# The first norm of a streaming-encoder block: products with diagonals of the tokens' factors in place of a scaled copy and transposes

## The chip, the core and the metric

The kernel runs on one core of one Trainium2 chip. The metric is the device time of one execution in microseconds (us), lower is better. A core has TensorE (PE, matrix products; its weight loads are shown as PEld), VectorE (DVE), ScalarE (ACT), GpSimd (POOL) and SyncE (SP, which here only issues DMAs). Each engine works through its own queue in order; semaphores tie them together.

## The reference

One layer of a hybrid encoder on 1024 tokens of 1024 channels, in float32:

```python
x = x + 0.5 * swiglu(rmsnorm(x, ffn1_norm), ffn1_w_gate, ffn1_w_up, ffn1_w_down)
# then a mixing block (gated gMLP heads and gated DeltaNet heads), added to x,
# a second SwiGLU half step, and a last RMSNorm
def rmsnorm(x, g):      # per token, over the 1024 channels
    return x * rsqrt(mean(x * x) + 1e-6) * g
def swiglu(x, w_gate, w_up, w_down):     # 2816 hidden channels
    return (silu(x @ w_gate) * (x @ w_up)) @ w_down
```

The change concerns the first `rmsnorm` and the way in which its result reaches the first `swiglu`. A norm has two kinds of factors: one for each token, `rsqrt(...)`, and one for each channel, `g`.

## The kernel before, in words

**The first FFN.** Products run on float32 data split into a high part, rounded to a shorter format (a cast on ACT), and a low part, the rest (a subtraction on DVE); three products of parts make one (`mm3`, line 55). The operands lie channel-major: 128 channels on the partitions, tokens along the row. The 2816 hidden channels are worked in 22 chunks of 128. Chunks 1 to 21 (`gu`, line 249) use a Strassen-like scheme with seven products in place of eight. Its blocks go by token halves and channel halves: the left half of the tokens are tiles 0 to 3 (a tile has 128 tokens), the right half tiles 4 to 7, and the channels are split at 512. So each product of such a chunk runs over four channel blocks k, on 512 columns. It needs, on the activation side, the blocks called B11, B21 and B22 and the sums T1 = B12 - B11, T2 = B22 - T1, T3 = T2 - B11 and T4 = B21 - T2, each as a high and a low part; on the weight side, four sums on POOL (`s1` to `s4`) and seven splits (`load_gu`, line 181). Chunk 0 (`gu_plain`, line 229) uses plain products on B11, B12, B21 and B22, without T sums, in two halves: columns 0 to 255 and columns 256 to 511. A column stands for one token of the left and one of the right half, so the first of these halves needs tiles 0, 1, 4, 5 and the second tiles 2, 3, 6, 7.

**The start of the program** is `start1` (line 467). For tiles 0, 4, 1, 5: ACT squares the tile and sums it along the row (line 74), DVE scales the sum and adds the epsilon (line 76), POOL takes the power -0.5 (line 70), and DVE multiplies the tile in place with the token factor and the norm row (line 82). The norm row is broadcast to 128 partitions by a DMA of 512 KB (`grow`, line 64). Then, for each pair of tiles (i, i + 4), `Combos.blocks` (line 127) transposes four channel blocks of 128x128 into one PSUM bank of 512 columns (`transposed`, line 92), four banks for each pair. From each bank ACT casts the high parts (lines 118 and 141), DVE subtracts for the low parts (lines 119 and 142), and unsplit copies for the T sums are taken off as well (lines 133, 137, 148, 150). The second half's norm treats its four tiles as one: four squares (line 488), one scaling (line 490), one power, four multiplies (line 493). At the end, `put_sums` (line 153) splits T2, T1, T3 and T4 for each of the four pairs: 16 casts of 128x512 on ACT, eight subtractions on DVE, eight on POOL, and four unsplit differences for T3 on POOL (line 157). After `start1`, the loop at line 311 prepares chunk 1's weights and runs it, and so on.

**What sets the order.** A scheduler that runs when the program is built fixes each engine's queue: written order gives the priority, and an instruction whose inputs it holds to be ready may pass one that is written earlier. Tiles of one tag share a number of buffers: the tag `x` has 8 (x tiles, later the unsplit f tiles, the gated hidden values and the loads of the down projection), `graw` 4 (raw gate and up weights), `gsp` 7 (split weights, B12, scratch), `sf` 4 (weight sums). PSUM has two sets of four banks, `mm` and `ax`. Chunk 0 uses `mm`, the transposes and chunk 1 use `ax`.

Of the kernel before, what the change touches and what calls it, by code (L numbers as in the profile page):

```python
# [30 lines left out]
def block_kernel(ctx: ExitStack, tc, a, out):  # L31
# [75 lines left out]
    class Combos:  # L107
        def __init__(self, g, qp, bp):
            self.g, self.qp, self.bp, self.B, self.f = g, qp, bp, {}, {}

        def put(self, n, i, src, eng):
# [5 lines left out]
            t = self.B[n][:, :, :, i * P:i * P + P]  # L117
            nc.scalar.copy(t[:, 0], src)  # L118
            eng.tensor_tensor(t[:, 1], src, t[:, 0], op=ALU.subtract)  # L119
# [7 lines left out]
        def blocks(self, i, pp, xns, uv, b12=None):  # L127
# [23 lines left out]
            yield  # L151

# [12 lines left out]
    def ffn(cb, wgu, wd, ps, rp, gp, qp, bp, start, load_xts, emit, before={}, fill=None):  # L165
# [145 lines left out]
        for c in range(1, NCH):  # L311
            together(load_gu(c))
            if c % 2:
                weight_sums(c // 2)
            else:
                hidden_sums(c // 2 - 1)
            gu(c, (A, X)[c % 2])
            for f in before.get(c, ()):
                f(xts)
# [125 lines left out]
    ba = cp.tile([P, 16, 8], F32, tag="ba", name="ba")[:, :8]  # L445
# [9 lines left out]
    xs = load_x(xdram, (0, 4))  # L455
    g = grow("ffn1_norm")
    xs.update(load_x(xdram, (1, 5)))

    with ExitStack() as f1:
# [5 lines left out]
        cb = Combos(g, qp, bp)  # L465

        def start1(f):
            def xi(i):
                return xs[i], xs[i + 4]

            uv = [cb.sums() for _ in range(2)]
            for j in range(2):
                for i in range(2):
                    normed(xi(i)[j], g, xi(i)[j], uv[i][j])
            def b12():
                return [f.gtile(F32R, "B12").rearrange("p s (k n) -> p s k n", k=2) for _ in range(2)]

            weights = f.load_gu(0, True)
            next(weights)
            xs.update(load_x(xdram, (2, 6, 3, 7)))  # L480
            b = b12()
            parts = [cb.blocks(i, f.X, xi(i), uv[i], b) for i in range(2)]
            together(*parts, n=2)
            together(*parts, weights)
            rest = xi(2) + xi(3)
            ms = sm.tile([P, 4], F32, tag="ssk", name="ms4")
            for i, x in enumerate(rest):
                nc.scalar.activation(f.gtile(F32, "junk").rearrange("p s n -> p (s n)"), x, AF.Square, accum_out=ms[:, i:i + 1])
            rs = sm.tile([P, 4], F32, tag="rk", name="rs4")
            nc.vector.tensor_scalar(rs, ms, 1.0 / D, EPS, op0=ALU.mult, op1=ALU.add)  # L490
            rpow(rs, rs, 4)
            for i, x in enumerate(rest):
                nc.vector.scalar_tensor_tensor(x, x, rs[:, i:i + 1], g, op0=ALU.mult, op1=ALU.mult)
            f.gu_plain(slice(0, 256), b)
            b = b12()
            for i in range(2, 4):
                together(cb.blocks(i, f.X, xi(i), cb.sums(xp), b))
            f.gu_plain(slice(256, 512), b)
            V, G = nc.vector, nc.gpsimd
            together(*(cb.put_sums(i, ("T2", "T1", "T3", "T4"), (V, G, V, G)) for i in range(4)))  # L500
# [57 lines left out]
    with ExitStack() as f2:  # L558
# [37 lines left out]
        cb = Combos(g2, qp, bp)  # L596
# [660 lines left out]
def _layout(np, x, ffn1_norm, ffn1_w_gate, ffn1_w_up, ffn1_w_down, mix_norm, w_in, gm_ln_g, gm_ln_b, gm_w_s,  # L1257
# [6 lines left out]
    def tmaj(cols):  # L1264
# [7 lines left out]
        x=x, ffn1_norm=ffn1_norm, mix_norm=mix_norm, ffn2_norm=ffn2_norm, final_norm=final_norm.reshape(1, D),  # L1272
# [34 lines left out]
```

## Time and profile before

| | |
|---|---|
| median of 3 timed runs | 1852.29 us (1849.4 to 1852.42) |
| the profiled execution | 1841.22 us, of which the profile's span is 1839.4 us |
| busy share of the span | PE 97%, DVE 65%, POOL 41%, ACT 37% |
| mean granted TensorE clock | 0.992 of full speed |
| moved by DMA | 302 MB, 164 GB/s on average |

Times in the profile are microseconds from the start of the span. A line such as L62 is a line of the kernel before; where it is that of a helper, the names of the written and read tiles tell the use: `out<-in`. "x1056" is a count. What follows a "|" in a group's row is busy time in us and the mean ns of one, then the engine's idle time just before them and what ended it. In rows of stretches, the numbers with (x...) are busy us and instructions of PE, PEld, DVE, ACT and POOL; then come the granted TensorE clock, the DMA engines' share and GB/s. In the chain of waits each row is a start, a length and what the time was spent on. The rows themselves are shown in the prediction.

### The profile page before, as it was taken

To read this page: it belongs to the slowest core of one execution; us is meant where nothing else is said; L and a number is where in the kernel's file an instruction comes from. 1 tells how busy PE (TensorE), PEld (TensorE's weight loads), DVE (VectorE), ACT (ScalarE), POOL (GpSimd) and SP (SyncE) were. 2 spreads that over 40 slices of the span, in tenths; PEclk is the share of its full clock that TensorE was granted. 3 is DMA by queue.
4 is the path that set the end of the run, shared out by engine and by line. 5 is a ranking of instruction groups with operands and counts; after the bars stand their busy time and mean duration, and the time that the engine had idled before them with its cause. 6 is when DMAs were issued, how large, how long until landed. Compare 5 with 4: busy or idle time off the path is not lost.

```text
span 1839.4 us, 25484 instructions
## 1 busy us (share of the span) xinstructions
PE 1784.1 (97%) x9735; PEld 1524.8 (83%) x9735; DVE 1191.7 (65%) x1531; ACT 686.6 (37%) x1193; POOL 747.9 (41%) x583
## 2 busy tenths in 40 slices
PE   5999999999999999898999999999999999999997
PEld 4888888888788889797788989988888888878886
DVE  6867676665565575769655344587776766656546
ACT  6333332333343454432344533452333323243433
POOL 4667666565140012212132420366666665614001
PEclk9999999999999999999999999999999999999999
DMA  5353443544957445453432254334535445495744
GB/s 196 108 175 136 162 152 134 184 158 163 339 188 258 155 177 164 140 195 100 133 94 67 90 197 136 109 104 165 178 132 171 144 154 188 142 344 185 264 142 149
DMA packets 134441, 302.26 MB, mean 164 GB/s; under 512 B 27408, under 2 KB 42032, under 8 KB 134320
## 3 DMA queue, kind: packets, MB, share of 16 engines
q1 hardware_dynamic: 131824, 296.20, 46.9%
q10 hardware_dynamic: 2496, 4.44, 0.8%
q8 instruction: 76, 1.25, 0.3%
q14 instruction: 45, 0.37, 0.1%
HBM read 208.83 MB, written 91.77 MB: 163 GB/s over the span
## 4 chain that ended last, share of the span: by engine, by line
PE 78%; DVE 8%; DMA 5%; POOL 4%; issue 3%; ACT 2%; SPq 0%; POOLq 0%; DVEq 0%; ACTq 0%
PE mm L53 43%; PE ax L53 32%; POOL s L191 1%; POOL t L278 1%; DMA left<-hq 1%; DVE acc L873 1%; PE ax L95 1%; PE sd L53 1%; DMA graw<-in_f1gu_dram 1%; POOL s L278 1%; PE sc L53 1%; DVE T L119 0%; DVE unit L62 0%; DVE wk L62 0%; DVE E L797 0%
## 5 line engine op out<-in xcount | busy, mean ns | idle before, releaser
L53 PE MATMUL mm<-unit 128*128 128x512 f32 x1056 | 244.9, 392 | 4.2 <-ACT unit L61 2.2
L53 PEld LDWEIGHTS mm<-unit 128*128 128x128 f32 x1056 | 198.8, 189 | 47.4 <-ACT unit L61 3.3
L191 POOL TENSOR_TENSOR s<-graw 128x512 f32<-128x512 f32 x84 | 130.3, 1551 | 262.9 <-DMA graw<-in_f2gu_dram 116.0
L62 DVE TENSOR_TENSOR ga<-graw,ga 128x512 fp32r<-128x512 f32 x134 | 155.9, 1166 | 99.9 <-ACT ga L61 99.2
L61 ACT CAST gs<-s 128x512 fp32r<-128x512 f32 x168 | 104.5, 622 | 301.8 <-PE mm L53 151.0
L62 DVE TENSOR_TENSOR unit<-left,unit 128x1024 fp32r<-128x1024 f32 x84 | 101.9, 1215 | 133.0 <-ACT unit L61 132.3
L53 PE MATMUL ax<-T,gs 128*128 128x512 f32 x792 | 183.1, 389 | 0.0
L53 PE MATMUL ax<-unit 128*128 128x512 f32 x792 | 180.5, 389 | 0.0
L53 PEld LDWEIGHTS ax<-T,gs 128*128 128x128 f32 x792 | 148.7, 188 | 30.8
L53 PEld LDWEIGHTS ax<-unit 128*128 128x128 f32 x792 | 148.7, 188 | 30.8
L62 DVE TENSOR_TENSOR gs<-s,gs 128x512 fp32r<-128x512 f32 x168 | 172.7, 1030 | 2.3
L53 PE MATMUL mm<-B,ga 128*128 128x512 f32 (+1 forms) x864 | 166.8, 347 | 3.3 <-ACT B L118 1.9
L61 ACT CAST unit<-left 128x1024 fp32r<-128x1024 f32 x84 | 82.5, 982 | 230.2 <-PE ax L53 100.5
L53 PE MATMUL mm<-T,gs 128*128 128x512 f32 x720 | 166.5, 389 | 0.0
L53 PEld LDWEIGHTS mm<-B,ga 128*128 128x128 f32 x864 | 139.5, 194 | 23.4 <-ACT B L118 2.5
L53 PEld LDWEIGHTS mm<-T,gs 128*128 128x128 f32 x720 | 135.2, 188 | 28.0
L70 POOL TENSOR_TENSOR rs<-rs,half 128x1 f32<-128x1 f32 (+1 forms) x29 | 19.2, 662 | 334.5 <-DVE rs L76 334.4
L53 PE MATMUL mm<-actT,wk 128*128 128x512 f32 x576 | 150.4, 403 | 0.0
L53 PE MATMUL ax<-B,ga 128*128 128x512 f32 x528 | 127.2, 390 | 1.4 <-DVE ga L62 1.4
L53 PE MATMUL mm<-wk,actT 128*128 128x256 f32 x960 | 123.5, 285 | 2.7 <-DVE wk L62 2.7
L53 PEld LDWEIGHTS mm<-wk,actT 128*128 128x128 f32 x960 | 117.4, 190 | 3.4 <-DVE wk L62 3.0
L53 PEld LDWEIGHTS mm<-actT,wk 128*128 128x128 f32 x576 | 103.6, 188 | 18.8
(239 smaller groups left out, 3046.0 us busy)
## 6 DMA issues: line engine op xcount, KB each, us to landing
left<-hq SPq DMA_DIRECT2D x70, 512.0 KB, 5.0
graw<-in_f1gu_dram SPq DMA_DIRECT2D x44, 512.0 KB, 5.4
wq<-t SPq DMA_DIRECT2D x44, 512.0 KB, 2.8
hq<-s SPq DMA_DIRECT2D x44, 512.0 KB, 3.1
graw<-in_f2gu_dram SPq DMA_DIRECT2D x44, 512.0 KB, 4.7
right<-wq SPq DMA_DIRECT2D x40, 512.0 KB, 4.8
wd<-in_f1wd_dram SPq DMA_DIRECT2D x22, 512.0 KB, 6.6
hq<-sg SPq DMA_DIRECT2D x22, 512.0 KB, 3.7
```

The costliest lines, as they stand in the source:

```text
L53: nc.tensor.matmul(*args, **kw)
L61: nc.scalar.copy(h, src)
L62: nc.vector.tensor_tensor(l, src, h, op=ALU.subtract)
L70: nc.gpsimd.tensor_tensor(o, i, half[:, :w], op=ALU.pow)
L95: nc.tensor.transpose(ps[:, i * P:(i + 1) * P], blk(i), ident)
L191: nc.gpsimd.tensor_tensor(f, u, v, op=op)
L278: nc.gpsimd.tensor_tensor(o, u, v, op=op)
L873: nc.vector.scalar_tensor_tensor(acc, pad[:, j:j + 512], cw[:, blk, j:j + 1], acc, op0=ALU.mult, op1=ALU.add)
```

## The change

For the first norm, the scaled copy of x and the transposes are left out. A product of a raw x block (128 tokens by 128 channels, as the stationary operand) with a diagonal matrix of 128 token factors yields the block transposed and scaled by token, in one step. The channel factors `g` now lie one to a partition after that product, so they are applied in the evictions from PSUM: ACT's cast gets a factor per partition (`nc.scalar.mul`), and DVE's subtraction becomes a multiply and subtract in one instruction (`scalar_tensor_tensor`).

- The norm's channel factors come as a 128x8 array (4 KB) in place of the row broadcast to 128 partitions.
- `factors` does four tiles at once for either half: four squares on ACT (with the 1/1024 folded into their scale), an add and a power on POOL, and four products of the identity with a token factor on DVE, which make the diagonals.
- `scaled_blocks` goes by channel blocks: for each of eight blocks, four products fill a bank with tiles 0, 1, 4, 5 (or 2, 3, 6, 7), and the evictions are 128x256: three casts or copies on ACT and three on DVE for blocks 0 to 3, two and four for blocks 4 to 7. Before, a bank held four channel blocks of one tile, and the evictions were 128x512.
- The second half's factors are asked for before chunk 0's products on the first half (before: four tiles' squares and power stood there too, with the four multiplies).
- The unsplit f tiles of the second half lie in three buffers of `x` and one of `graw`.
- `scaled_sums` makes the T sums for 256 columns at once: eight casts of 128x1024 (as 4x256) in place of 16 of 128x512, and likewise the subtractions.
- Chunk 1's weights (`load_gu(1)`) are prepared in turns with the T sums; before, they followed them.

```diff
+        def scaled_blocks(self, i, pp, xts, dg, g, f, b12):
+            sl = slice(i * 256, i * 256 + 256)
+            t3, t1, t2, t4 = self.f[i] = f
+            def less(o, src, c, v):
+                nc.vector.scalar_tensor_tensor(o, src, g[:, c:c + 1], v, op0=ALU.mult, op1=ALU.subtract)
+            def put(h, l, src, c):
+                nc.scalar.mul(h, src, g[:, c:c + 1])
+                less(l, src, c, h)
+            for c in range(8):
+                ps = bank(*pp)
+                for n, x in enumerate(xts):
+                    mm(ps[:, n * P:n * P + P], x[:, c * P:c * P + P], dg[:, n * P:n * P + P], start=True, stop=True)
+                u, v = ps[:, :256], ps[:, 256:]
+                k = c % 4
+                if c < 4:
+                    b = self.block("B11")
+                    put(b[:, 0, k, sl], b[:, 1, k, sl], u, c)
+                    nc.scalar.mul(t3[:, k], u, g[:, c:c + 1])
+                    b = b12[k // 2]
+                    put(b[:, 0, k % 2], b[:, 1, k % 2], v, c)
+                    less(t1[:, k], v, c, t3[:, k])
+                else:
+                    b = self.block("B21")
+                    put(b[:, 0, k, sl], b[:, 1, k, sl], u, c)
+                    b = self.block("B22")
+                    put(b[:, 0, k, sl], b[:, 1, k, sl], v, c)
+                    less(t2[:, k], v, c, t1[:, k])
+                    less(t4[:, k], u, c, t2[:, k])
+                yield
+        def scaled_sums(self, i, names, engs):
+            t3, t1, t2, t4 = self.f[i]
+            for n, eng in zip(names, engs):
+                if n == "T3":
+                    nc.gpsimd.tensor_tensor(t3, t2, t3, op=ALU.subtract)
+                src, t = {"T1": t1, "T2": t2, "T3": t3, "T4": t4}[n], self.block(n)[:, :, :, i * 256:i * 256 + 256]
+                nc.scalar.copy(t[:, 0], src)
+                eng.tensor_tensor(t[:, 1], src, t[:, 0], op=ALU.subtract)
+                yield
...
         for c in range(1, NCH):
-            together(load_gu(c))
+            if c not in gu_s:
+                together(load_gu(c))
...
-    xs = load_x(xdram, (0, 4))
-    g = grow("ffn1_norm")
-    xs.update(load_x(xdram, (1, 5)))
+    nc.scalar.dma_start(g1, a["f1g"])
+    xs = load_x(xdram, (0, 1, 4, 5))
...
-            for j in range(2):
-                for i in range(2):
-                    normed(xi(i)[j], g, xi(i)[j], uv[i][j])
...
+            order = ((0, 1, 4, 5), (2, 3, 6, 7))
+            def factors(ts):
+                ms, rs = (sm.tile([P, 4], F32, tag=n, name=n) for n in ("ssk", "rk"))
+                for n, t in enumerate(ts):
+                    junk = f.gtile(F32, "junk").rearrange("p s n -> p (s n)")
+                    nc.scalar.activation(junk, xs[t], AF.Square, scale=D ** -0.5, accum_out=ms[:, n:n + 1])
+                nc.gpsimd.tensor_scalar(rs, ms, EPS, None, op0=ALU.add)
+                rpow(rs, rs, 4)
+                dg = rp.tile([P, 544], F32, tag="sf", name="dg", bufs=4)[:, :512]
+                for n in range(4):
+                    nc.vector.tensor_scalar(dg[:, n * P:n * P + P], ident, rs[:, n:n + 1], None, op0=ALU.mult)
+                return dg
...
             weights = f.load_gu(0, True)
+            dg = factors(order[0])
             next(weights)
-            xs.update(load_x(xdram, (2, 6, 3, 7)))
+            xs.update(load_x(xdram, order[1]))
             b = b12()
-            parts = [cb.blocks(i, f.X, xi(i), uv[i], b) for i in range(2)]
-            together(*parts, n=2)
-            together(*parts, weights)
-            rest = xi(2) + xi(3)
...
-            for i, x in enumerate(rest):
-                nc.vector.scalar_tensor_tensor(x, x, rs[:, i:i + 1], g, op0=ALU.mult, op1=ALU.mult)
+            together(cb.scaled_blocks(0, f.X, [xs[t] for t in order[0]], dg, g1, four(cb.sums() + cb.sums()), b), weights)
+            dg = factors(order[1])
             f.gu_plain(slice(0, 256), b)
             b = b12()
-            for i in range(2, 4):
-                together(cb.blocks(i, f.X, xi(i), cb.sums(xp), b))
+            t4 = rp.tile([P, 1088], F32, tag="graw", name="t4", bufs=4)[:, :D].rearrange("p (a n) -> p a n", a=2)
+            fs = four([xp.tile([P, 2, 512], F32, tag="x", name="f") for _ in range(3)] + [t4])
+            together(cb.scaled_blocks(1, f.X, [xs[t] for t in order[1]], dg, g1, fs, b))
             f.gu_plain(slice(256, 512), b)
             V, G = nc.vector, nc.gpsimd
-            together(*(cb.put_sums(i, ("T2", "T1", "T3", "T4"), (V, G, V, G)) for i in range(4)))
+            together(f.load_gu(1), *(cb.scaled_sums(i, ("T2", "T1", "T3", "T4"), (V, G, V, G)) for i in range(2)))
```

Blank lines of the diff are left out here. The second FFN's norm keeps the scaled copy, the transposes and the T sums as they are.

More of the change, by code (lines that the diff above doesn't have):

```diff
@@ L107, in block_kernel, with __init__, block @@
     class Combos:
-        def __init__(self, g, qp, bp):
-            self.g, self.qp, self.bp, self.B, self.f = g, qp, bp, {}, {}
-        def put(self, n, i, src, eng):
+        def __init__(self, qp, bp):
+            self.qp, self.bp, self.B, self.f = qp, bp, {}, {}
+        def block(self, n):
             if n not in self.B:
@@ L116, in put @@
                     self.B[n] = act_tile(name=n)
-            t = self.B[n][:, :, :, i * P:i * P + P]
+            return self.B[n]
+        def put(self, n, i, src, eng):
+            t = self.block(n)[:, :, :, i * P:i * P + P]
             nc.scalar.copy(t[:, 0], src)
@@ L444, in block_kernel @@
     sp = {n: dr.tile([8, P, 512], F32, tag="sp" + n, name="sp" + n) for n in "zvm"}
-    ba = cp.tile([P, 16, 8], F32, tag="ba", name="ba")[:, :8]
+    ba = cp.tile([P, 16, 8], F32, tag="ba", name="ba")
+    g1 = ba[:, 8]
+    ba = ba[:, :8]
     def load_x(src, ts):
@@ L464, in block_kernel @@
         bp = pool(f1, "bp")
-        cb = Combos(g, qp, bp)
+        cb = Combos(qp, bp)
         def start1(f):
-            def xi(i):
-                return xs[i], xs[i + 4]
-            uv = [cb.sums() for _ in range(2)]
-            for j in range(2):
-                for i in range(2):
-                    normed(xi(i)[j], g, xi(i)[j], uv[i][j])
+            order = ((0, 1, 4, 5), (2, 3, 6, 7))
[10 more added lines that the diff above has]
+                return dg
@@ L475, in b12, with four @@
             def b12():
                 return [f.gtile(F32R, "B12").rearrange("p s (k n) -> p s k n", k=2) for _ in range(2)]
+            def four(ts):
+                return [t.rearrange("p a (b n) -> p (a b) n", b=2) for t in ts]
             weights = f.load_gu(0, True)
+            dg = factors(order[0])
             next(weights)
-            xs.update(load_x(xdram, (2, 6, 3, 7)))
+            xs.update(load_x(xdram, order[1]))
             b = b12()
-            parts = [cb.blocks(i, f.X, xi(i), uv[i], b) for i in range(2)]
@@ L483, in start1 @@
-            together(*parts, n=2)
-            together(*parts, weights)
-            rest = xi(2) + xi(3)
-            ms = sm.tile([P, 4], F32, tag="ssk", name="ms4")
-            for i, x in enumerate(rest):
[L488 to L491, printed above, removed]
@@ L492, in start1 @@
-            for i, x in enumerate(rest):
-                nc.vector.scalar_tensor_tensor(x, x, rs[:, i:i + 1], g, op0=ALU.mult, op1=ALU.mult)
+            together(cb.scaled_blocks(0, f.X, [xs[t] for t in order[0]], dg, g1, four(cb.sums() + cb.sums()), b), weights)
+            dg = factors(order[1])
             f.gu_plain(slice(0, 256), b)
             b = b12()
-            for i in range(2, 4):
-                together(cb.blocks(i, f.X, xi(i), cb.sums(xp), b))
+            t4 = rp.tile([P, 1088], F32, tag="graw", name="t4", bufs=4)[:, :D].rearrange("p (a n) -> p a n", a=2)
@@ L594, in w_out @@
                 yield
-        cb = Combos(g2, qp, bp)
+        cb = Combos(qp, bp)
         pp = (ps[1], "ax")
@@ L1271, in _layout @@
     m = dict(
-        x=x, ffn1_norm=ffn1_norm, mix_norm=mix_norm, ffn2_norm=ffn2_norm, final_norm=final_norm.reshape(1, D),
+        x=x, f1g=ffn1_norm.reshape(KC, P).T, mix_norm=mix_norm, ffn2_norm=ffn2_norm, final_norm=final_norm.reshape(1, D),
         f1gu=gu(ffn1_w_gate, ffn1_w_up), f1wd=ffn1_w_down.reshape(NCH, P, D),
```

## The prediction

> **What bounds the kernel now.** I read the page first, then busy time by stretches, then the chain of waits, then the timeline of the first 70 us. The page's engine line says that TensorE (PE) is busy throughout.
>
> ```profile
> PE 1784.1 (97%) x9735; PEld 1524.8 (83%) x9735; DVE 1191.7 (65%) x1531; ACT 686.6 (37%) x1193; POOL 747.9 (41%) x583
> ```
>
> The change touches only what comes before the second channel chunk of the first FFN, so the stage matters. Busy time by stretches (first the length, then each engine's busy us, then the granted TensorE clock):
>
> ```profile
> 10.00:20.00 10.00, 6.95 (x31) 5.45 (x30) 8.33 (x13) 6.42 (x14) 1.62 (x3) 1.00 0.99 398
> 20.00:30.00 10.00, 9.41 (x78) 9.06 (x77) 9.54 (x14) 9.94 (x21) 7.74 (x6) 1.00 0.15 54
> 30.00:40.00 10.00, 4.86 (x35) 4.48 (x34) 6.50 (x5) 4.47 (x10) 7.24 (x6) 0.84 0.15 52
> 40.00:50.00 10.00, 7.30 (x32) 6.23 (x31) 9.55 (x17) 7.02 (x15) 4.42 (x4) 0.50 0.37 130
> 60.00:70.00 10.00, 8.58 (x41) 6.90 (x40) 10.00 (x11) 2.62 (x5) 7.62 (x6) 1.00 0.43 157
> 70.00:80.00 10.00, 10.00 (x45) 8.28 (x45) 8.00 (x10) 3.37 (x6) 5.70 (x4) 1.00 0.27 88
> ```
>
> From 70 us on PE has no gap; between 30 and 50 it is half idle and its clock drops to 0.50, while VectorE (DVE) is nearly full. The chain of waits over the first 100 us names what PE stood behind (start, length, what):
>
> ```profile
> 28.61 4.20 POOL s L191 x3
> 32.82 0.99 POOL rs L70
> ...
> 36.03 0.91 DVE x L493
> ...
> 38.24 2.47 DVE x L493 x2
> ...
> 51.80 6.16 DVE T L119 x6
> ...
> 60.86 1.77 DVE ga L62
> 62.63 0.04 issue
> 62.67 18.89 PE ax L53 x82
> 81.56 18.59 PE mm L53 x82
> ```
>
> The second half's token factors wait for GpSimd (POOL), which is in the next chunk's weight sums (L191); then DVE multiplies four x tiles (L493); later it is behind T subtractions (L119) when chunk 1 wants its weights (L62). At 62.67 the dense stream begins, and it sets the end: whatever moves 62.67 moves the end by as much. That is my yardstick.
>
> **The change part by part.** Removed: eight 128x1024 multiplies on DVE, the broadcast load of the norm row, and the transposes. Rows of the first 80 us and of the whole run (count, busy us, mean ns of one):
>
> ```profile
> L82 DVE SCALAR_TENSOR_TENSOR x<-x,rs,grow 128x1024 f32<-128x1024 f32 x4 | 5.0, 1283 | 3.4 <-DMA grow<-in_ffn_norm_dram 2.1 <-POOL rs L70 1.3
> L493 DVE SCALAR_TENSOR_TENSOR x<-x,rs,grow 128x1024 f32<-128x1024 f32 x4 | 6.9, 1777 | 3.5 <-POOL rs L70 3.5
> L119 DVE TENSOR_TENSOR B<-ax,B 128x512 fp32r<-128x512 f32 x12 | 7.9, 680 | 0.4 <-ACT B L118 0.4
> L142 DVE TENSOR_TENSOR B<-ax,B 128x256 fp32r<-128x256 f32 x8 | 3.2, 417 | 0.8 <-ACT B L141 0.7
> L1025 DVE TENSOR_TENSOR u<-u,sc 128x128 f32<-128x128 f32 x32 | 9.1, 286 | 17.3 <-PE sc L53 16.1 <-ACT u L994 1.1
> L1032 DVE SCALAR_TENSOR_TENSOR S<-S,ex,sd 128x128 f32<-128x128 f32 x32 | 11.1, 346 | 12.1 <-PE sd L53 11.5
> L871 DVE TENSOR_SCALAR acc<-pad,cw 128x512 f32<-128x512 f32 x24 | 11.6, 482 | 13.3 <-ACT pad L869 13.2
> ```
>
> DVE, evictions. Before: 24 subtractions of 512 (12 for B, 12 for the f tiles, alike) and 8 of 256: 24 x 0.68 + 8 x 0.417 = 19.7 us. After: per half 3 for each of four channel blocks and 4 for each of four others, 56 of 128x256 with a factor per partition. That form is not in the trace at 256. A 128x128 with such a factor takes 346 against 286 without: +60 ns, so 0.417 + 0.06 = 0.477 each, 26.7 us (bounds 0.417 and 0.53, twice the surcharge: 23.4 to 29.7; I take 26.7, since the pointer is there). So +7.0. The multiplies give back 5.0 + 6.9 = 11.9. The diagonals are 8 products of 128x128 with a per-partition factor; by L871 they cost less than 0.48, and at half of that or so 0.24 each: 1.9 (bounds 1.2, by the 150 ns of a one-column operation of L76 below, and 3.9). Net on DVE: -3.0.
>
> PE. The 64 products replace 64 transposes.
>
> ```profile
> 751.98 1.06 PE L53 MATMUL sc<-kst 128*128 128x128 f32 x8
> 1077.18 0.60 PE L95 MATMUL ax<-ident,ya 128*128 128x128 f32 x4
> L53 PE MATMUL sc<-kst 128*128 128x128 f32 x32 | 4.2, 275 | 0.0
> L95 PE MATMUL ax<-ident,ya 128*128 128x128 f32 x32 | 5.0, 280 | 0.2
> 48.31 12.46 PE L53 MATMUL mm<-B,ga 128*128 128x256 f32 x94
> ```
>
> Eight full-precision products of this shape in a row take 1.06, so one each (1.06 - 0.275) / 7 = 0.112 us; four transposes (0.60 - 0.280) / 3 = 0.107. The exchange costs 64 x 0.005 = 0.3 us. PE's whole work ahead of chunk 1 is 64 x 0.112 + 192 x 12.46 / 94 = 7.2 + 25.4 = 32.6 us at this clock.
>
> The Trainium skill's page "TensorE: Matmul & The Clock Gate" (section Terms) credits the transpose mode with being 4x faster for FP32, which speaks against this exchange: by it the products would add 64 x 3 x 0.107 = 20.5 us. The two rows disagree with it, and I go by them; the case stands below as a rival.
>
> ScalarE (ACT).
>
> ```profile
> L896 ACT ACTIVATE kst<-ax 128x128 f32<-128x128 f32 x32 | 8.4, 276 | 2.6 <-PE ax L844 2.6
> L1027 ACT ACTIVATE oh<-sq,ex 128x128 f32<-128x128 f32 x32 | 11.8, 368 | 16.4 <-PE sq L53 16.0
> L141 ACT CAST B<-ax 128x256 fp32r<-128x256 f32 x8 | 2.8, 385 | 1.6 <-DVE f L137 1.6
> 11.98 0.19 ACT L74 ACTIVATION_READ_ACCUMULATOR f<-x 128x1 f32 x1
> L76 DVE TENSOR_SCALAR rs<-ms 128x1 f32<-128x1 f32 x4 | 0.5, 150 | 5.7 <-ACT f L74 5.7
> L657 POOL TENSOR_SCALAR rs<-rs 128x1 f32<-128x1 f32 x1 | 0.2, 190 | 0.1
> L70 POOL TENSOR_TENSOR rs<-rs,half 128x4 f32<-128x4 f32 x1 | 1.0, 1024 | 0.0
> ```
>
> 40 evictions with a factor, each 0.385 + (0.368 - 0.276) = 0.477: 19 us over some 35, with four squares beside them. ACT stays the lesser load, but not by much.
>
> Start. The four squares still end ACT's first stretch at 11.98 + 0.19 = 12.2 (the x tiles come at the latest as now; leaving out the 512 KB norm row can only help). Then POOL's add 0.19, power 1.02, a diagonal 0.24 and some 0.15 of handover: the first product starts at about 13.8. The first transposes now come earlier, but FFN products wait for all four tiles there too.
>
> Second half. Its factors are now asked for ahead of the first half's products. The squares, then add and power, lie behind ACT and POOL work of the first half with some 15 us of cover; if that cover fails, see the first rival. No DVE instruction stands between square and power any more, and products and evictions work by channel blocks for 256 tokens at once, so PE can multiply with block k while DVE works on the next.
>
> When chunk 1 can start. By PE: 13.8 + 32.6 + 3 for a cold clock at the start (an estimate: 6 us at half rate, under half of the 0.50 stretch above) + 1.5 waiting for the first evicted block = 50.9. By DVE: 13.8 + 1.9 + 26.7 + 3.7 (three of the four weight splits of chunk 0 at 1.24, row below; one falls into the wait before 13.8) + 1.7 (4 SwiGLU products of 256, like L142) = 47.8, and 1.6 for the last twelve products = 49.4 (bounds 45.4 to 54.4, from those above). The later is 50.9; two nearly full engines never mesh wholly, so I add 1.1: 52.0.
>
> Moved loads and sums. Chunk 1's weight preparation moves ahead of the T sums and alternates with them: 2 DMAs on the SP queue, 7 casts on ACT, 7 splits on DVE, 4 sums on POOL. No DMA was queued between old and new place, so the SP queue keeps its order; but one of the four weight buffers now holds t4, so chunk 1's second load waits for a buffer of chunk 0, free by about 30, with 15 us to spare, and chunk 2's second load waits for the last T4 subtraction, about 57, with some 7 us to spare. The T sums are half as many and twice as wide:
>
> ```profile
> L119 DVE TENSOR_TENSOR T<-f,T 128x512 fp32r<-128x512 f32 x8 | 10.6, 1380 | 0.0
> L62 DVE TENSOR_TENSOR unit<-left,unit 128x1024 fp32r<-128x1024 f32 x70 | 90.5, 1294 | 107.1 <-ACT unit L61 106.3 <-DMA hq<-sg 0.6
> L62 DVE TENSOR_TENSOR ga<-graw,ga 128x512 fp32r<-128x512 f32 x9 | 11.0, 1237 | 1.1 <-ACT ga L61 1.1
> ```
>
> Four of 1024 on DVE cost 4 x 1.29 to 4 x 2.76 (5.2 to 11.0) for 10.6 now. Chunk 1's first product no longer waits behind them: its split comes first. But its fourth product (T3) has four T subtractions and four splits ahead: from 47.8 that is 5.2 to 11.0 + 4 x 1.24 + two evictions of 0.68 = 59.3 to 65.1, and PE wants it at 52 + 3 x 2.8 = 60.4 (2.8: 18.89 us of chunk 1 over nearly seven products). A stall of 0 to 4.7; with POOL half busy I take 1.3.
>
> **Sum:** the equivalent of 62.67 becomes 52.0 + 1.3 = 53.3, so 9.4 us earlier. The profiled execution took 1841.2 (span 1839.4 and 1.8 around it) and would take 1831.8; the timed runs lie 11 us higher, at a median of 1852.3, and the gain is the same in both: 1852.3 - 9.4 = **1842.9**.
>
> The same page of the Trainium skill (Part 1) says that an idle window of about 3.4 us halves the PE clock, and a busy one restores it. The 0.50 row agrees: it follows the gap between these rows, 32.7 to 36.26, and full rate returns only with the dense stretch that begins at 48.31.
>
> ```profile
> 29.22 3.48 PE L53 MATMUL mm<-B,ga 128*128 128x256 f32 x27 [0.59 <-DVE ga L62]
> 36.26 0.63 PE L95 MATMUL ax<-ident,x 128*128 128x128 f32 x4 [3.56 <-DVE x L493]
> ```
>
> By the page's 3.4 us window the cold start would cost 1.7, not 3: 1.3 us better.
>
> **Rivals.** *The second factors come late again.* POOL takes what is ready; three weight sums (4.20 in the chain) or a double-width T sum can stand ahead of the add and power. Then DVE idles some 5 us between halves and the clock falls again, 1.5 more: gain 2.9, 1849.4. For it: just that happened before; against: POOL has less to do by then, and the DVE step is gone. *The blocks run in lockstep* (slower): if a product group, its casts, its subtractions and the next group don't overlap, a block costs 0.6 + 3 or 2 x 0.48 + at most 4 x 0.48, say 3.1; 16 blocks are 49.6 from 13.8, with 1.6 of products and 2.0 of chunk 1's wait 67.0, so 4.3 later: 1856.6. It becomes slower from 2.8 us a block. Against: four PSUM banks, and now eight banks of the second half pass between 36.26 and 51.8, 1.94 each with T work among them. *The products cost four transposes*: +20.5 on PE, hardly hidden, 1863; the rows speak against it. *Better than forecast*: PE fills its waits with chunk 1's first product and no T stall: 48.5, so 14.2 earlier, 1838.1.
>
> **Chances.** Forecast 0.60 (by itself 1839 to 1847), late factors 0.16, lockstep 0.10, dear products 0.02, better 0.12. The range 1837 to 1853 leaves out the slower cases and a tail below. A measurement tells 0.2% (3.7 us) from no change. Faster: 0.60 + 0.12 + a third of 0.16 = 0.77; same: the rest of 0.16 and a little of lockstep, 0.12; slower 0.11.
>
> **What will show it.** Chunk 1's dense stream starts at 52 to 55; the first product at 13.8; products of 128x128 on diagonals at 0.11 us apart once warm; evictions of 256 near 0.48 on DVE and ACT; the second half's power before 32; no 0.50 stretch from 37 to 50. I'm wrong if PE still idles over 3 us between halves, if DVE's 56 subtractions take over 0.53 each, or if PE stalls over 5 us within chunk 1.

## The result: 0.65% slower

The changed kernel takes 1862.5 us (median of 20 runs, 1856.5 to 1865.7) against 1849.0 for the kernel before in the same session (20 runs, 1842.7 to 1865.7). The ratio is 1.0065, 95% interval 1.0049 to 1.0081: some 12 us slower (13.5 by the medians), where 9.4 us faster was forecast. The profiled execution took 1861.8 us (span 1859.7). New names used below: L163 is DVE's multiply and subtract, L166 and L178 ACT's scaled casts and copies, L196 the T3 difference, L198 and L199 cast and subtraction of the T sums, L234 the raw weight loads, L240 POOL's sums of raw weights, L327 its sums of down weights, L342 a write of the down projection's operands, L313 an eviction of chunk 1, L531 the diagonals.

Busy time by stretches, changed kernel (columns as in the prediction):

```profile
30.00:40.00 10.00, 7.27 (x52) 6.69 (x51) 9.62 (x11) 5.68 (x8) 7.42 (x4) 0.93 0.00 1
40.00:50.00 10.00, 10.00 (x79) 9.85 (x78) 8.72 (x20) 7.63 (x19) 1.08 (x1) 0.89 0.04 12
60.00:70.00 10.00, 8.67 (x39) 6.79 (x38) 10.00 (x7) 4.43 (x8) 10.00 (x6) 1.00 0.22 80
70.00:80.00 10.00, 3.92 (x18) 2.91 (x16) 3.93 (x4) 0.00 (x0) 3.69 (x4) 0.81 0.64 205
```

The half-idle stretch between 30 and 50 is mostly mended, as meant: PE is busy 7.27 of 10 from 30 to 40 (before 4.86) and full from 40 to 50 (before 7.30). A new hole stands from 70 to 80, where all four engines are idle most of the time and DMA is at 205 GB/s. The timeline of PE shows it exactly (start, length, what, and the idle time before it with its releaser):

```profile
13.38 7.03 PE L53 MATMUL ax<-dg,x 128*128 128x128 f32 x40 [13.38 <-DVE dg L531]
...
38.50 4.79 PE L53 MATMUL ax<-dg,x 128*128 128x128 f32 x26 [1.81 <-DVE dg L531]
...
58.46 2.92 PE L53 MATMUL ax<-B,ga 128*128 128x512 f32 x12
...
63.18 8.02 PE L53 MATMUL ax<-T,gs 128*128 128x512 f32 x34 [1.33 <-DVE gs L62]
71.04 2.88 PE L53 MATMUL ax<-B,ga 128*128 128x512 f32 x12
83.44 4.42 PE L53 MATMUL ax<-B,gs 128*128 128x512 f32 x12 [9.52 <-DVE pe L313]
87.70 2.89 PE L53 MATMUL ax<-T,ga 128*128 128x512 f32 x12
90.42 2.88 PE L53 MATMUL mm<-B,ga 128*128 128x512 f32 x12
```

Chunk 1 starts at 58.46 (forecast 52.0). Its sixth product then waits 9.52 us, and the twelve matmuls after the wait take 4.42 instead of 2.88 at a lowered clock (0.68 from 80 to 90). In what follows **M** is the start of chunk 2's first product in the timeline of PE, from which on PE is dense again: 81.40 before, 90.42 after, 9.0 later. (The chain of waits in the prediction, which counts to the end of chunk 1's last matmul, has 81.56 for it.) The chain of waits names what the 9.52 us consist of:

```profile
54.00 1.73 POOL f L196
...
58.20 6.08 POOL s L240 x3
64.28 1.70 POOL t L327
65.98 2.80 POOL T L199
68.78 3.40 POOL t L327 x2
72.20 0.37 SPq L342
...
72.67 5.61 DMA graw<-in_f1gu_dram
...
78.44 1.23 POOL s L240
...
81.04 0.63 ACT gs L61
81.72 0.98 issue
82.71 0.69 DVE pe L313
```

Read it backwards. The eviction L313 that PE needs stands on DVE behind a split of chunk 2's weights (81.72). That waits for POOL's sums (78.44), those for chunk 2's raw weights, landed at 78.3. The load was issued only at 72.67, because SP's queue stood at the instruction ahead of it, a write whose data came from POOL's last down-weight sum (72.20). And POOL is full from 54 to 72. The SP queue shows both ends:

```profile
48.88 0.91 SPq L234 DMA_DIRECT2D graw<-in_f1gu_dram  x2
...
66.00 6.57 SPq L342 DMA_DIRECT2D wq<-t  x2
72.67 1.80 SPq L234 DMA_DIRECT2D graw<-in_f1gu_dram  x3
```

Chunk 1's raw weights are asked for at 48.88 (in the kernel before, they and chunk 2's were asked for between 8.9 and 29.6): t4, the fourth f tile, takes its turn in the same four buffers ahead of them (it is written at 48.86). In SP's queue the loads go out right behind a load for the down projection (L334, at 48.51), for which the queue had waited 34.4 us on PE; with the raw loads written ahead of t4 (e1 below) they go out at 9.88, ahead of that load. So chunk 1's four weight sums fall between 56.4 and 64.3, into the stretch where POOL makes T sums and down-weight sums.

### The profile page after: what moved, and what is told of

It is laid out like the page before. It is cut to its first block, busy times and chain, and to the rows that moved or that the text cites. A ratio compares the mean times of both kernels' runs of the same rounds, so it can differ in the third digit from the quotient of the medians.

```text
span 1859.7 us, 25631 instructions
## 1 busy us (share of the span) xinstructions
PE 1797.4 (97%) x9799; PEld 1538.4 (83%) x9799; DVE 1164.5 (63%) x1546; ACT 690.1 (37%) x1201; POOL 739.4 (40%) x576
## 4 chain that ended last, share of the span: by engine, by line
PE 76%; DVE 7%; POOL 6%; DMA 4%; issue 4%; ACT 2%; SPq 0%; POOLq 0%; DVEq 0%; ACTq 0%
PE mm L53 43%; PE ax L53 31%; POOL s L240 2%; POOL t L327 1%; DMA graw<-in_f1gu_dram 1%; DVE acc L927 1%; POOL s L327 1%; PE sd L53 1%; DMA graw<-in_f2gu_dram 1%; PE sc L53 1%; PE ax L95 1%; DMA left<-hq 0%; DVE unit L62 0%; DVE wk L62 0%; DVE o L82 0%
## 5 line engine op out<-in xcount | busy, mean ns | idle before, releaser
L240 POOL TENSOR_TENSOR s<-graw 128x512 f32<-128x512 f32 x84 | 131.8, 1569 | 272.2 <-DMA graw<-in_f1gu_dram 116.1
L62 DVE TENSOR_TENSOR ga<-graw,ga 128x512 fp32r<-128x512 f32 x134 | 143.1, 1071 | 115.9 <-ACT ga L61 115.3
L62 DVE TENSOR_TENSOR gs<-s,gs 128x512 fp32r<-128x512 f32 x168 | 180.3, 1075 | 10.7 <-ACT gs L61 8.4
L53 PEld LDWEIGHTS ax<-T,gs 128*128 128x128 f32 x792 | 148.6, 188 | 32.6 <-DVE gs L62 1.8
L70 POOL TENSOR_TENSOR rs<-rs,half 128x1 f32<-128x1 f32 x24 | 16.0, 666 | 324.7 <-DVE rs L76 324.6
```

The costliest lines, as they stand in the source:

```text
L53: nc.tensor.matmul(*args, **kw)
L62: nc.vector.tensor_tensor(l, src, h, op=ALU.subtract)
L70: nc.gpsimd.tensor_tensor(o, i, half[:, :w], op=ALU.pow)
L240: nc.gpsimd.tensor_tensor(f, u, v, op=op)
```

## Experiments

All ratios are to the kernel before in the same session, with 95% intervals. "Waits" are those of PE within chunk 1.

| kernel | chunk 1 starts | waits | M | ratio |
|---|---|---|---|---|
| before | 60.6 | 1.42 | 81.40 | 1 |
| after | 58.5 | 1.33, 9.52 | 90.42 | 1.0065 [1.0049, 1.0081] |
| e1 after, raw loads ahead of t4 | 60.9 | 0.72, 2.97 | 85.91 | 1.0045 [1.0022, 1.0069] |
| e2 after, move undone | 58.7 | 1.32, 8.99 | 90.50 | 1.0065 [1.0044, 1.0086] |
| e3 before, one f tile in a raw buffer | 55.9 | 2.71 | 79.59 | 0.9987 [0.9962, 1.0012] |
| e4 after, diagonals on ACT | 55.5 | 1.34, 9.54 | 87.62 | 1.0028 [1.0004, 1.0052] |
| e5 after, t4 in the norm row's buffer | 60.1 | 0.72, 2.17 | 84.36 | 1.0038 [1.0009, 1.0066] |
| e6 e5 and e4 | 60.3 | 0.78, 2.20 | 83.00 | 1.0035 [1.0016, 1.0053] |
| e7 e6, T sums in pieces of 512 | 57.1 | 1.12 | 77.64 | 1.0010 [0.9990, 1.0030] |
| e8 before, move alone | 60.6 | none | 79.67 | 0.9987 [0.9966, 1.0007] |
| e9 e7, transposes for products | 46.1 | 2.02, 1.28, 2.85 | 75.00 | 0.9959 [0.9944, 0.9974] |
| e10 x scaled, then transposed | 52.5 | 2.85, 2.85, 0.47 | 81.88 | 1.0007 [0.9987, 1.0028] |
| e11 e8, add on POOL | 60.2 | 0.19 | 79.79 | 0.9985 [0.9965, 1.0004] |
| e12 after, T sums in pieces of 512 | 60.8 | 0.90, 0.40, 3.44 | 87.08 | 1.0042 [1.0025, 1.0059] |
| e13 after, T sums on DVE | 52.5 | 2.60, 2.91 | 79.25 | 1.0000 [0.9982, 1.0018] |
| e14 e7, T sums on DVE | 52.6 | 0.31, 0.94 | 73.81 | 0.9997 [0.9977, 1.0017] |
| e15 e10, T sums on DVE | 51.5 | 1.40, 0.70, 0.77, 0.65 | 79.00* | 0.9973 [0.9942, 1.0005] |
| e16 e8, T sums on DVE | 54.4 | none | 73.47 | 0.9975 [0.9947, 1.0003] |
| e17 the same, more rounds | 54.0 | none | 73.09 | 0.9997 [0.9971, 1.0022] |
| e18 before, T sums on DVE | 54.7 | 1.76, 1.90 | 79.71 | 0.9988 [0.9975, 1.0000] |

\* Five of this product's twelve matmuls ran earlier, among those of chunk 1, so it isn't comparable as it stands.

### The buffer, the move, the diagonals (e1 to e4)

```diff
 e1: raw1 = f.raws(1)               # right after the second half's x loads
     together(f.load_gu(1, raw=raw1), *(cb.scaled_sums(...
 e2: -together(f.load_gu(1), *(cb.scaled_sums(...
     +together(*(cb.scaled_sums(...
 e3: in the kernel before, one f tile of the last pair:
     +rp.tile([P, 1088], F32, tag="graw", name="f3", bufs=4)
 e4: -nc.vector.tensor_scalar(dg[...], ident, rs[:, n:n + 1], None, op0=ALU.mult)
     +nc.scalar.mul(dg[...], ident, rs[:, n:n + 1])
```

> The changed kernel with one difference: chunk 1's two raw weight tiles are asked for before the f tile t4, so t4 takes its turn in the four raw-weight buffers behind them. Theory A (the turn of t4 holds chunk 1's loads back to 48.9 us, POOL's weight sums with them, and through the SP queue chunk 2's loads): chunk 1's loads go out near 10 us, the 9.5 us gap of PE ahead of chunk 1's sixth product is gone or under 3 us, chunk 2's first product moves from 90.4 to 78 to 82, and the ratio to the kernel before falls from 1.0065 to between 0.998 and 1.002. Theory C (the preparation of chunk 1 in turns with double-width T sums overloads POOL and DVE, wherever the loads are): the gap stays over 5 us and the ratio over 1.004.

> The changed kernel with chunk 1's weight preparation put back behind the T sums. Theory A: the loads still stand behind t4 and the wd load in the SP queue, so the gap in chunk 1 stays at 8 us or more and the ratio to the kernel before is 1.005 to 1.009. Theory C: the gap shrinks below 5 us and the ratio is 1.003 or less.

> The kernel before with one difference: the last of the second half's f tiles lies in one of the four raw-weight buffers, as t4 does in the changed kernel. Theory A: chunk 1's loads slip from 9 us to 40 or later, behind the wd loads, PE gets a gap of 5 us or more within chunks 1 and 2, and the ratio is 1.003 to 1.008 although products, evictions and sums are those of before. Theory C, or any theory by which the new products and evictions cost the time: within 0.2% of the kernel before.

> The changed kernel with the diagonals made on ACT in place of DVE. Theory B (a DVE product of the identity with a token factor waits for a POOL instruction of 2.4 us to end; three such waits delay the second half by 6 to 7 us): the second half's products run from 33 us on without the waits at 35.6 and 36.7, and chunk 1's first product comes at 52 to 54 instead of 58.5. Theory A on top of it: the loads still set chunk 2's start through the SP queue, so most of this is given back, the gap within chunk 1 grows, and the ratio stays at 1.003 to 1.006; if B were all, the ratio would fall by 0.003 or more with the gap unchanged.

With the raw weights asked for early (e1) the long wait falls from 9.52 to 2.97 and M by 4.5, to 85.91, where theory A had 78 to 82. The move of chunk 1's weights is not the cause (e2 is the changed kernel again). Late loads need not do harm by themselves: e3 holds chunk 1's back to 34.9 in the kernel before and loses nothing there. (It even starts chunk 1 4.7 earlier: with no raw weights to sum, POOL takes the second half's power at 28.92 instead of 32.77.) Whether loads at 48.9 would do harm there isn't tested; what else the long wait needs comes with e13 below. e4 leaves the long wait and takes 3.0 off the start of chunk 1, and M falls by 2.8. The diagonals had cost more than 0.24 us each in the second half. The timelines of DVE, then POOL, in the changed kernel:

```profile
30.38 2.42 DVE L531 TENSOR_SCALAR dg<-ident,rk 128x128 f32<-128x128 f32 x1 [0.38 <-POOL rk L70]
...
33.51 0.27 DVE L531 TENSOR_SCALAR dg<-ident,rk 128x128 f32<-128x128 f32 x1
...
34.10 4.35 DVE L531 TENSOR_SCALAR dg<-ident,rk 128x128 f32<-128x128 f32 x2
```

```profile
30.32 2.40 POOL L199 TENSOR_TENSOR T<-f,T 128x1024 fp32r<-128x1024 f32 x1
33.66 2.40 POOL L196 TENSOR_TENSOR f<-f 128x1024 f32<-128x1024 f32 x1 [0.95 <-DVE f L163]
36.01 2.35 POOL L199 TENSOR_TENSOR T<-f,T 128x1024 fp32r<-128x1024 f32 x1
```

The one diagonal that falls between two POOL instructions (33.51) takes 0.27. The others end with the POOL instruction that runs beside them: at 32.80 (POOL 32.72), and two at 38.45 (POOL 36.06 and 38.36). L163, which reads PSUM, keeps its 0.47 us in between. The Trainium skill says, in "Trainium Architecture — The Big Picture" (What this means for kernel authors), that DVE and GpSimd contend for a shared port pair by an exclusive lock; these rows agree.

### The buffer given back, and the width of the T sums (e5 to e7, e12)

```diff
 e5: -t4 = rp.tile([P, 1088], F32, tag="graw", name="t4", bufs=4)[:, :D]
     +t4 = cp.tile([P, D], F32, tag="grow", name="t4")      # the norm row's, free now
 e7, e12: in scaled_sums, difference, cast and subtraction
     +for k in (slice(0, 2), slice(2, 4)):                  # 512 columns at a time
```

> The changed kernel with the f tile t4 in the norm row's buffer (free until the mixing norm's row is loaded) in place of a raw-weight buffer. Theory A in the form that the first runs leave (t4 keeps a raw-weight buffer until its last subtraction at 66 to 69 us, so a load of chunk 2 comes after it, POOL's and DVE's work for chunk 2 stands waiting in the queues ahead of chunk 1's, and PE with them): chunks 1 and 2 are loaded by 30 us, PE's gap ahead of chunk 1's sixth product (9.5 us; 3.0 with chunk 1 alone loaded early) is under 1 us, its cold products go, chunk 2's first product comes at 79 to 82 (before 81.6, changed 90.4), ratio to the kernel before 0.997 to 1.002. Theory C (double-width sums on POOL and their order set the gap): gap over 3 us, chunk 2 at 84 or later.

> The last kernel, and the diagonals made on ACT. Theory A with B: 3 us better than the last kernel, as in the run with ACT's diagonals alone: chunk 1's first product at 54 to 57, chunk 2's at 75 to 79, ratio 0.994 to 1.000. If A fails, the gap within chunk 1 takes back what the second half gains and chunk 2's first product stays after 82.

> The same, with each T sum made in two pieces of 128x512, as wide as in the kernel before. Theory C: shorter POOL pieces (1.3 instead of 2.4 us) let the others in between, chunk 2's first product comes 2 us or more earlier than in the last kernel. Theory A: width does not matter, within 1 us of the last kernel.

> The changed kernel with nothing but the T sums in pieces of 512. Theory C (width): POOL, ACT and DVE wait less for each other, chunk 2's first product comes 4 us or more earlier than 90.4, with t4 still in the raw-weight buffer. Theory A (t4's buffer alone decides how late chunk 2's load is): within 2 us of 90.4, the gap ahead of chunk 1's sixth product stays over 7 us.

Without t4 among the raw weights (e5) the long wait is 2.17, so the buffer is needed for the 9.52; M is 84.36, where theory A had 79 to 82. But chunk 1 now starts later (60.1 instead of 58.5), and e4's edit gains only 1.4 more. What is left goes with the width: pieces of 512 take 5.4 off M (e6 to e7) and 3.3 off that of the changed kernel (e12), though the columns worked on are the same. In e6 the first evictions of the second half stand on ACT behind a T3 cast that waits for a POOL difference of 2.34 us.

### Products against transposes, and the moves in the kernel before (e8 to e11)

```diff
 e8:  in the kernel before: +together(f.load_gu(1), *(cb.put_sums(...
 e9:  -mm(ps[...], x[:, c * P:c * P + P], dg[:, n * P:n * P + P], start=True, stop=True)
      +nc.tensor.transpose(ps[...], x[:, c * P:c * P + P], ident)
 e10: e9, without diagonals, x scaled in place (first half DVE, second half ACT):
      +nc.scalar.mul(xs[t], xs[t], rs[:, n:n + 1])
 e11: e8 with scale=D ** -0.5 in the squares and
      +nc.gpsimd.tensor_scalar(rs, ms, EPS, None, op0=ALU.add)
```

e9 leaves the token factors out of the result; it is there to price the products. e10 computes the whole norm.

> The kernel before, with chunk 1's weight preparation put in turns with the T sums and nothing else. Theory A: no harm, since the loads stay where they are; the wait of 2.1 us for chunk 1's first weight split shrinks, ratio 0.997 to 1.001. Theory C: a gap of over 3 us appears within chunk 1, ratio over 1.002.

> The kernel with t4 in the norm row's buffer, diagonals on ACT and T sums in pieces of 512, with a transpose by the identity in place of each product with a diagonal; the token factors are thereby left out of the result, all else runs as before. Theory D (a full-precision product is two matrix instructions of 0.112 us, a transpose is one of 0.107, so the 64 products cost PE 7.5 us more, and PE bounds the time up to chunk 1): chunk 1's first product comes at 50 to 54 instead of 57.1, chunk 2's at 71 to 75 instead of 77.6, ratio 0.995 to 0.999. Rival (DVE and ACT bound that stretch, PE's extra work is hidden): chunk 1's first product moves by less than 1.5 us.

> A full kernel by theory D: the token factors are applied to x in place (first half on DVE, second half on ACT), then blocks are transposed, channel factors stay in the evictions, no diagonals; t4 in the norm row's buffer and T sums in pieces of 512. Theory D: PE saves 7.5 us as in the run with bare transposes; the scaling costs 2 to 3 us ahead of the first transpose and up to 2 us between halves; chunk 1's first product at 53 to 57, chunk 2's at 74 to 78, ratio 0.996 to 1.000. Rival: the scaling of 1024 columns stands in the way as much as before, no gain over the kernel that it comes from (ratio 1.001 or more).

> The kernel before, with chunk 1's preparation in turns with the T sums and the second half's epsilon added on POOL in place of DVE. My theory of the wait between halves (the power at 32.8 stands behind DVE's scaling at 29.1 and three weight sums on POOL): the power comes by 30.5, the second half 2 us earlier, ratio 0.996 to 0.999. Rival: the power's place in POOL's queue stays behind the weight sums, no change from the move alone (0.9987).

PE's timeline in e9:

```profile
46.07 2.91 PE L53 MATMUL ax<-B,ga 128*128 128x512 f32 x12
...
51.45 5.50 PE L53 MATMUL ax<-T,gs 128*128 128x512 f32 x23 [2.02 <-DVE gs L62]
58.24 0.49 PE L53 MATMUL ax<-T,gs 128*128 128x512 f32 x1 [1.28 <-DVE T L200]
```

Chunk 1 starts 11.0 earlier than in e7 (57.08), M comes 2.6 earlier, and the ratio falls by 0.0051 (9.4 us, more than M accounts for). The products are dear, but the 11.0 isn't their price alone: with no token factors to wait for, 16 transposes run before 9.7, where e7's first product starts at 11.56. The group of the products in the changed kernel, and the page's line of the engines, say why:

```profile
L53 PE MATMUL ax<-dg,x 128*128 128x128 f32 x128 | 20.1, 322 | 15.8 <-DVE dg L531 15.8
```

```profile
PE 1797.4 (97%) x9799; PEld 1538.4 (83%) x9799; DVE 1164.5 (63%) x1546; ACT 690.1 (37%) x1201; POOL 739.4 (40%) x576
```

128 matmuls for 64 products, and 64 more on PE in all (9799 after, 9735 before): a full-precision product is issued as two. At the prediction's 0.112 each that is 14.3 us where it had 7.2, and 7.5 more than 64 transposes at 0.107. The Trainium skill's "TensorE: Matmul & The Clock Gate" (Terms) has transposes 4x faster for FP32; here it is 2 x 0.112 against 0.107, twice. e10 scales x, as the kernel before does: chunk 1 still starts 4.6 earlier than in e7, but waits of 6.2 in it give that back (M 81.88). The move alone (e8) helps by 1.7 of M, since chunk 1's first split no longer stands behind T subtractions; the add's place (e11) does nothing.

### POOL against DVE (e13 to e18)

In e9 and e10 chunk 1 starts early and then waits mostly for splits on DVE that stand in a row of instructions of 1.5 to 1.75 us. Still open then: does the long wait hang on the buffer, on POOL's length, or on what POOL does to DVE?

```diff
 e13 to e16, e18: all of the first norm's T sums on DVE
 -nc.gpsimd.tensor_tensor(t3, t2, t3, op=ALU.subtract)
 +nc.vector.tensor_tensor(t3, t2, t3, op=ALU.subtract)
 -("T2", "T1", "T3", "T4"), (V, G, V, G)
 +("T2", "T1", "T3", "T4"), (V, V, V, V)
```

> The changed kernel with one edit: the T4 and T1 subtractions and the T3 differences of the first norm's T sums (six instructions of 128x1024, about 2.4 us each on POOL) go to DVE, so all T sums' subtractions are there. Theory S (POOL and DVE stand in each other's way: a DVE instruction of 128x512 on SBUF operands alone takes 0.68 us, beside a running POOL instruction 1.5 to 1.8): POOL loses 14 us of work between 48 and 72, DVE gains at most 6 x 1.28 = 7.7 and its own ten or so instructions there fall by 0.7 to 1.0 each; the 9.5 us stall falls below 5 us and chunk 2's first product comes at 84 to 87 instead of 90.4; time 1855 to 1859. Theory R (only the late raw buffer counts, POOL's length does not): the stall stays at 8 to 10 and the time at 1861 to 1864. Theory W (DVE is the fuller engine and takes on 7.7 us): chunk 2's first product later than 92, 1865 or more.

> The kernel with t4 in the norm row's buffer, diagonals on ACT and T sums in pieces of 512, with the T4 and T1 subtractions and T3 differences moved from POOL to DVE (twelve of 128x512). Theory S: DVE's pieces fall from a mean of 1.34 to about 0.7 to 0.9, so 20 instructions cost 14 to 18 where 8 + 8 cost 22 before; PE has no wait in chunk 1, chunk 2's first product comes at 75.5 to 77 (77.6 before), 1845 to 1848. Theory W: DVE's eight more microseconds push the splits of chunk 1 back, PE waits 3 us or more in chunk 1, chunk 2's first product at 80 or later, 1851 or more.

> The kernel that scales x in place and transposes it, with the T4 and T1 subtractions and T3 differences moved from POOL to DVE. Before the edit PE waits twice 2.85 us for a split of chunk 1 (DVE) that stands behind T subtractions of 1.5 to 1.75 us each. Theory S: these fall to 0.7 to 0.9, the two waits together to under 2.5 us, chunk 2's first product comes at 77 to 79 instead of 81.9, 1845 to 1848. Theory W: the waits grow to more than 6 us together, chunk 2's first product at 83 or later, 1852 or more.

> The kernel before with chunk 1's weights in turns with the T sums, and the T4 and T1 subtractions and T3 differences moved from POOL to DVE. Theory S: chunk 1 starts at 60.6 as without the edit (the second half is bound by other things up to there), the T subtractions fall from 1.41 to 0.7 to 0.9 us, nothing waits in chunk 1, chunk 2's first product at 79 to 80: the time is that without the edit, 1844 to 1847. Theory W: DVE has no room from 50 to 80 (10.00 of 10 busy in each stretch), PE waits 2 us or more for a split or an eviction in chunk 1, chunk 2's first product at 82 or later, 1849 or more.

e13 keeps the buffer, the products, the width, the diagonals on DVE and the move, and takes only POOL out of the T sums. M falls by 11.2, more than by any other single edit (theory S had said 3 to 6), and the ratio from 1.0065 to 1.0000 (0.9982 to 1.0018): all that the change had lost. Chunk 1 starts 6.0 earlier, of which e4 puts 3.0 on the diagonals, which nothing on POOL holds up now (group below), and the two waits sum to 5.5 instead of 10.9. PE has no wait at all from its first product at 13.47 to 52.47, so its own work ahead of chunk 1 is 39.0 us, where the prediction had 32.6. The buffer is as it was, and chunk 1's loads still go out at 45.3: most of what it cost goes with POOL's T sums, but not all. The wait of 2.60 ends with a cast that waits for POOL's weight sums, and these wait until 52.0 for the raw weights. The group of the diagonals in e13, then its timelines, PE, DVE and POOL:

```profile
L531 DVE TENSOR_SCALAR dg<-ident,rk 128x128 f32<-128x128 f32 x8 | 1.9, 282 | 12.6 <-POOL rk L70 12.6
```

```profile
52.47 0.63 PE L53 MATMUL ax<-B,ga 128*128 128x512 f32 x2
...
66.84 4.38 PE L53 MATMUL ax<-T,gs 128*128 128x512 f32 x11 [2.91 <-DVE T L199]
...
79.25 2.88 PE L53 MATMUL mm<-B,ga 128*128 128x512 f32 x12
```

```profile
56.00 3.49 DVE L62 TENSOR_TENSOR gs<-s,gs 128x512 fp32r<-128x512 f32 x2
59.41 2.32 DVE L196 TENSOR_TENSOR f<-f 128x1024 f32<-128x1024 f32 x1
...
65.58 1.21 DVE L199 TENSOR_TENSOR T<-f,T 128x1024 fp32r<-128x1024 f32 x1
...
67.31 0.68 DVE L62 TENSOR_TENSOR gs<-s,gs 128x512 fp32r<-128x512 f32 x1
```

```profile
62.84 1.74 POOL L327 TENSOR_TENSOR t<-wd,t 128x512 f32<-128x512 f32 x1
69.80 1.28 POOL L240 TENSOR_TENSOR s<-graw 128x512 f32<-128x512 f32 x1 [5.23 <-DVE ga L62]
```

POOL works to 64.6 and again from 69.8. Beside it DVE's instructions of 512 take 1.75 each (3.49 for two) and those of 1024 take 2.3; between 65.6 and 69.8, where POOL is idle, the same forms take 0.68 and 1.21. POOL's own 512 takes 1.28 alone and 1.74 beside DVE. So a pair, one on each engine side by side, takes about 1.75 us, and both one after the other on DVE 1.36. Giving half of the T sums to POOL is dearer than keeping them.

In e14 M falls by 3.8. In e15, where M can't be compared, chunk 2's fifth product starts at 87.39 instead of 92.76 in e10, 5.4 earlier, though the waits in chunk 1 still sum to 3.5. The same edit in the kernel before with the move (e16) brings M to 73.47, 7.9 earlier than before, with no wait in chunk 1. Theory S had chunk 1 start at 60.6 there, as without the edit; it starts at 54.4. Groups of e16, 20 to 85 us:

```profile
L119 DVE TENSOR_TENSOR T<-f,T 128x512 fp32r<-128x512 f32 x16 | 11.4, 751 | 0.0
...
L494 DVE SCALAR_TENSOR_TENSOR x<-x,rs,grow 128x1024 f32<-128x1024 f32 x4 | 4.9, 1282 | 0.9 <-POOL rs L70 0.9
```

Sixteen T subtractions take 11.4 us on DVE where eight took 10.6 (1380 each), the multiplies of the second half 1282 where they took 1777, and the wait for the factors 0.9 where it was 3.5. Two more runs test it:

> The same kernel as in the run before of that name, in more rounds: the kernel before, chunk 1's weights in turns with the T sums, and the T sums' work moved from POOL to DVE. By its trace chunk 2's first product comes at 73.5, 8.1 us earlier than in the kernel before (81.6), while its median was 5.8 us lower. If the earlier start counts, the ratio's interval lies below 1: 0.996 to 0.998. If the gain of that run was the scatter of its runs, the ratio is 0.999 to 1.001.

> The kernel before with the T4 and T1 subtractions and T3 differences of the first norm moved from POOL to DVE, and chunk 1's weights left where they are. If the shorter POOL queue is what helps (the second half's power at 28.8 instead of 32.7, the four multiplies on DVE at 1.28 instead of 1.78 us), chunk 1's first product comes at 54 to 56 and chunk 2's first at 73.5 to 77, ratio 0.996 to 0.999. If the move of chunk 1's weights is needed as well, chunk 1 starts early and then PE waits for the split of its second product or later, 2 us or more, and chunk 2's first product stays at 79 or later, ratio 0.999 to 1.001.

Both parts are needed: without the move (e18) chunk 1 starts early and waits 1.76 and 1.90. But e17's ratio is 0.9997, though M stands at 73.09. Its twelve runs lie in two groups: seven from 1837.7 to 1847.1, five from 1853.5 to 1857.0, and the profile is of the second. Busy time by stretches, e17 and then e16, and the row of PE in e17 ahead of it:

```profile
890.00:900.00 10.00, 8.58 (x62) 5.82 (x61) 2.30 (x5) 1.51 (x4) 0.10 (x1) 0.67 0.37 99
900.00:910.00 10.00, 10.00 (x61) 7.55 (x60) 4.68 (x8) 2.62 (x5) 0.00 (x0) 0.50 0.10 18
910.00:920.00 10.00, 10.00 (x46) 7.84 (x46) 1.21 (x3) 0.95 (x2) 0.00 (x0) 0.50 0.46 138
```

```profile
890.00:900.00 10.00, 10.00 (x112) 7.53 (x113) 5.30 (x11) 3.49 (x8) 0.00 (x0) 1.00 0.40 107
```

```profile
891.92 0.41 PE L53 MATMUL ax<-Z,L 32*32 32x32 f32 x8 [1.42 <-DMA Z<-xz]
```

Some 800 us behind the change PE waits for a small transfer, 1.42 us here and 0.86 in e16; then the clock stays at half for about 25 us, and the time is 13 us longer from there on (from 836 to 1099 in e17 and from 835 to 1085 in e16). So e16 and e17 show a gain of 8 us in the stage, and none of the whole time that can be told from no change; e14, with M at 73.81 and 0.9997, is alike. Where the clock doesn't fall the gain does reach the end: over the sessions of e16 and e17, runs with a mean granted clock of 0.986 or more have a median of 1842.7 (15 of 22), those of the kernel before 1849.4 (44 of 52), by a division made after the fact. Whether an earlier M makes that fall likelier isn't known. Nor does the length of the wait decide it: at the same place the clock falls for some 10 us in e5, behind a wait of 0.99, and stays full behind 1.17 in the kernel before and 1.36 in e15.

## Why the prediction was wrong

By the forecast's own steps M would have been 53.3 + 18.7 = 72.0 (18.7: from 62.67 to 81.40 before). It was 90.4, 18.4 later: 6.5 from the start of chunk 1 (58.5, not 52.0), 9.5 from the long wait, 1.5 from the lowered clock after it. Of the 0.9 that is left, 0.5 is a slip of the yardstick: 62.67 is chunk 1's third matmul, and 52.0 stands for its first.

- **"The exchange costs 64 x 0.005 = 0.3 us": the step that failed first.** The rows for the price were read as one matmul each; the row "x8" held four products of two matmuls. The term comes to 14.3 and not 7.2 us of PE, and in e13, without a wait, PE's work ahead of chunk 1 takes 39.0 us and not 32.6. With it, "by PE" gives 13.4 + 39.7 + 3 + 1.5 = 57.6 against 58.46 measured, but that is in part luck: e13 does the same work and starts chunk 1 at 52.47. The other 6.0 are PE's waits between the halves (2.7, of which 2.4 for diagonals) and the lower clock there (0.93 and 0.89 from 30 to 50, in e13 1.00), not a cold start. This is the rival of dear products, at twice a transpose instead of four times; that its 1863 meets the measured 1862.5 is chance, since the products account for some 7 us and not 20.5.
- **"The diagonals ... 0.24 each": right for the first half, wrong for the second.** There four take 7.0 us, because POOL's T sums run beside them. e4 prices it at 3 us; with POOL out of the way (e13) all eight take the 1.9 us of the forecast. The bound of 0.48 was taken from a row of another stage, and what POOL does beside it wasn't looked at.
- **"Moved loads and sums ... 15 us to spare ... some 7 us to spare": the step that cost most.** That chunk 1's second load waits for a buffer of chunk 0 was looked at, not that both loads, written behind t4, could end up in SP's queue behind a load that waits until 48.5, nor that the write L342 ahead of chunk 2's load waits for POOL. From the load at 72.67 to the eviction at 82.71 lie ten microseconds that the forecast had nowhere. e1 and e5 take 6.6 and 7.4 of the 9.5 away.
- **"Four of 1024 on DVE cost 5.2 to 11.0 for 10.6 now": in the range (6.3), but the wrong engine.** The width cost its time on POOL, where one instruction blocks the queue, and DVE, for 2.4 us. That POOL's half of the T sums slows DVE's was to be seen in the rows quoted (1380 ns for T, 680 for the same size read from PSUM) and was taken for DVE's own price. e13 shows that this is where all of the measured loss can be had back.
- **Right:** the first product (13.4 for 13.8), the evictions (477 and 474 ns for 477 on DVE, 495 and 479 on ACT), the second half's power before 32 (29.3), no 0.50 stretch from 37 to 50. The stall of 1.33 for 1.3 is luck: the forecast had it at the fourth product (T3), behind T subtractions, and it came in the second (T2), behind the split of a weight. "I'm wrong if PE stalls over 5 us within chunk 1" is what came.

The rest of the difference, some 3 us between the shift of M (9.0) and that of the time (12), isn't settled, but it arises later, in stages that the change doesn't touch: in the two profiled executions the shift is still 9.1 at the first product behind the chunks (464.3 and 473.4) and 13.6 at the first product with `wo` (1081.0 and 1094.7). Over the kernels of the table the time differs from M's shift by -3 to +8 us. The clock falls later in the program, as in e17, are one source of that.

## What to carry to other kernels

Price an operation by counting instructions in the trace, not products in the source. When a mean duration has several values in one kernel, find what ran beside it before using it: two engines that slow each other are not two engines, and work taken off the "idle" one can be worth more than any trimming of the full one. When a tile is put into a rotating buffer, write down what has to come after it in turn, and follow each queue that then stands.

## What the runs showed of the hardware

- DVE on SBUF operands and POOL slow each other: 0.68 to 1.75 us for 128x512 on DVE, 1.28 to 1.74 on POOL; a one-operand product of 128x128 waits for the whole POOL instruction (0.27 to 2.42).
- A full-precision product of 128x128 is two matmuls of 0.112 us, a transpose one of 0.107.
- At one place of the program the clock fell to 0.50 for some 25 us behind a wait of 1.42 us (e17) and for some 10 us behind 0.99 (e5), and stayed full behind 0.86 (e16), 1.17 (before) and 1.36 (e15). The length of the wait alone doesn't decide it; what does isn't shown.
